# A weight split with every second low half made by an accumulating transfer: one decoder layer on one core

## The chip, the core and the metric

The kernel runs on one core of a Trainium2 chip. Its engines have queues of their own: TensorE (PE, with the weight loads shown apart as PEld), VectorE (DVE), ScalarE (ACT), GpSimd (POOL) and SyncE (SP), and 16 DMA engines serve the core. The metric is the device time of one execution in microseconds, as the median of the runs shown.

## What is computed

One layer of a decoder on x (256 positions, 2048 channels), all in float32:

```python
z = x @ w_in + b_in                      # 2048 x 15368
zu, zv, zqk, zvm, zo, zi, zf, zqx, zg = jnp.split(z, IN_OFFSETS, axis=-1)
y_a = chunked_spatial_gating(gelu(zu), gelu(zv), ...)
y_b = sigmoid(zo) * head_norm(mlstm(silu(conv(zqk)), zvm, zi, zf)) * m_norm_g
y_c = memory_cross_attention(zqx, mem_n @ x_w_kv)
merged = sum(sigmoid(zg_i) * (y_i @ w_pi) for i in (a, b, c))
x = layer_norm(ALPHA * x + merged @ w_out, ln1_g, ln1_b)
gate, up = jnp.split(x @ w_gu, 2, axis=-1)   # d_ff = 5632
x = layer_norm(ALPHA * x + (silu(gate) * up) @ w_down, ln2_g, ln2_b)
```

Nearly all of the work is products of the 256 positions with large weight matrices, some 331 MB of weights in float32.

## The kernel before

**Split products.** Each float32 operand of a large product is split into a high half in the format fp32r and a low half, the rest, in fp32r too. A product is then three: high by high, high by low, low by high. Activations are split once, where they are made. Weights are split as they stream in.

**Pieces and jobs.** All weights are cut into pieces of 256 rows by 512 columns, held as a tile of 128 x 1024 (512 KB). A job is one block of 512 columns: 4, 8 or fewer pieces, summed in PSUM, then evacuated. There are 632 pieces in one list, numbered through in the order of the jobs. In form A (`mul_a`, L1018) the weights are stationary: for each half `hf` four matmuls of the high half over both activation halves (L1024), then four of the low half over the high activations (L1026). In form B (`mul_b`, L1002) the weights move: for each of two row blocks and two channel blocks a matmul with the high half (L1014), one with the low half (L1015), one with the high half again (L1016). So the low half is wanted first behind four matmuls in form A, behind one in form B.

**The stream.** The order on each engine is the program's own. The loop over the pieces (L1092) calls, for piece i, `advance` (loads up to eight pieces ahead, L951, from SP), `advance_split` (the high half of piece i+4 and the low half of piece i+3), `mults(i)`, and at a job's end its evacuation; in between `run_side` adds steps of the side tasks (memory norm, gating, attention, mLSTM). A raw tile (`raw`, 6 buffers) is split in two instructions: `split` copies it to the high half `wh` on ScalarE (L979, 5 buffers), `split_lo` subtracts the high half from it on VectorE into `wl` (L994, 4 buffers). A high half can be made once the matmuls of the piece five before are done; then its buffer is free.

**Around it.** Evacuations (`comb`, L585, and the `ev_` functions) alternate between ScalarE and VectorE, and splits of new activations (`split_from`, L184) do too: ScalarE copies, VectorE subtracts. The high halves stand in ScalarE's queue behind these. GpSimd makes constants at the start, one mask (L282), and four small fills (L673). The output projection's last block and the last down projection (`late`) run one row block over their last pieces first, then the other, so that the row norms (`RowNorm`) can start; the last of their pieces have buffers of their own (`own`).

Of the kernel before, what the change touches and what calls it, by code (L numbers as in the profile page):

```python
# [12 lines left out]
F32R = mybir.dt.float32r  # L13
I32 = mybir.dt.int32
AF = mybir.ActivationFunctionType
ALU = mybir.AluOpType
# [3 lines left out]
P = 128  # L20
# [5 lines left out]
H = 4  # L26
ALPHA = 2.0 ** 0.25
EPS = 1e-5
RAW_BUFS = 6
HL_BUFS = 4  # L30
SPLIT_AHEAD = 3
LOAD_AHEAD = 8
SIDE_NS = 1000
VERBOSE = False
W0, W1 = 7, 14
# [53 lines left out]
def layer_kernel(ctx: ExitStack, tc: tile.TileContext, xT_d, mem_d, memT_d, wi_d, wif_d, wkv_d,  # L89
                 wpa_d, wpb_d, wpc_d, wout_d, wgu_d, wdn_d, pp_d, bif_d, gws_d, gbs_d, bin_d, gln_d, xr_d, lnp_d, out_d):  # L90
    nc = tc.nc
    ve, ac, te, gp, sy = nc.vector, nc.scalar, nc.tensor, nc.gpsimd, nc.sync
# [4 lines left out]
    wp = ctx.enter_context(tc.tile_pool(name="wp", bufs=HL_BUFS))  # L97
# [7 lines left out]
    def nm(s):  # L105
        cnt[0] += 1
        return f"{s}{cnt[0]}"

    def slot(tag, shape, dt=F32):
        return big.tile(shape, dt, tag=tag, name=nm(tag))  # L110
# [73 lines left out]
    def split_from(src, hi_ap, lo_ap):  # L184
        ac.activation(hi_ap, src, AF.Copy)  # L185
        ve.tensor_sub(lo_ap, src, hi_ap)  # L186
# [19 lines left out]
    def run_side(budget):  # L206
        held = False
        for t in list(tasks):
            if not t.free:
                if held:  # L210
                    continue
                held = True
            while budget > 0:
                try:
                    c = next(t.gen)
                except StopIteration:
                    tasks.remove(t)
                    break
                if c == WAIT:
                    break  # L220
                budget -= c
            if budget <= 0:
                break
# [723 lines left out]
    raw, hl, owned, cur = {}, {}, {}, [0]  # L947
# [3 lines left out]
    def load(i):  # L951
        job, k = pieces[i]
        r = wp.tile([P, 1024], F32, tag="raw", name=nm("raw"), bufs=RAW_BUFS)
        raw[i] = r
        if i == 0:
            for j in range(2):
                sy.dma_start(xraw[:, j], xT_d[:, j])
                sy.dma_start(r[:, j * 512:(j + 1) * 512], job.src[k][:, j * 512:(j + 1) * 512])
            return
        if i < nx:  # L960
            sy.dma_start(xraw[:, 2 * i:2 * i + 2], xT_d[:, 2 * i:2 * i + 2])
        sy.dma_start(r, job.src[k])
        if k == 0 and job.bias is not None:
            job.bc = bc2()
            o = job.bias
            sy.dma_start(job.bc, bin_d[0:1, o:o + 512].to_broadcast([P, 512]))

    def split(i):
        job, k = pieces[i]
        r = raw[i]  # L970
        if k in job.own:
            tag, m = job.own[k]
            if m == 0:
                S["own"] = slot(tag, [P, 2, 2, 1024], F32R)
            h = S["own"][:, m, 0]
            owned[i] = S["own"][:, m, 1]
        else:
            h = wp.tile([P, 1024], F32R, tag="wh", name=nm("wh"), bufs=HL_BUFS + 1)
        ac.activation(h, r, AF.Copy)  # L979
        hl[i] = [h, None]  # L980

    def split0():
        r = raw.pop(0)
        h = wp.tile([P, 1024], F32R, tag="wh", name=nm("wh"), bufs=HL_BUFS + 1)
        l = wp.tile([P, 1024], F32R, tag="wl", name=nm("wl"))
        hl[0] = [h, l]
        for j in range(2):
            o = slice(j * 512, (j + 1) * 512)
            split_from(xraw[:, j], xT.one(j, 0), xT.one(j, 1))
            split_from(r[:, o], h[:, o], l[:, o])  # L990

    def split_lo(i):
        l = owned.pop(i) if i in owned else wp.tile([P, 1024], F32R, tag="wl", name=nm("wl"))
        ve.tensor_sub(l, raw.pop(i), hl[i][0])  # L994
        hl[i][1] = l

# [67 lines left out]
    def advance(i):  # L1064
        while state["ld"] < min(N, i + LOAD_AHEAD + 1) and state["ld"] < state["sp"] + RAW_BUFS:
            load(state["ld"])
            if state["ld"] == 2:
                sy.dma_start(pp, pp_d)
            state["ld"] += 1

    def advance_split(i):
        while state["sp"] < min(N, i + SPLIT_AHEAD + 1):
            k = state["sp"]
            while state["hi"] < min(N, k + 2):
                if state["hi"] == 0:
                    split0()
                else:
                    if state["hi"] < nx:
                        xsplit_hi(state["hi"])
                    split(state["hi"])  # L1080
                state["hi"] += 1
            if k > 0:
                if k < nx:
                    xsplit_lo(k)
                split_lo(k)
            state["sp"] += 1
            advance(i)
# [4 lines left out]
    for i in range(N):  # L1092
        job, k = pieces[i]
# [13 lines left out]
        else:  # L1107
            run_side(SIDE_NS)

# [61 lines left out]
```

## Time and profile before

| | |
|---|---|
| median of three runs | 1864.68 us (1863.83 to 1866.85) |
| the profiled execution: its own time | 1864.04 us |
| span in the profile, first to last instruction | 1862.3 us |
| PE busy | 1840.6 us |
| VectorE busy | 1148.7 us |
| ScalarE busy | 898.4 us |
| GpSimd busy | 4.4 us |
| mean granted clock of TensorE | 0.996 |
| DMA | 351.53 MB, mean 189 GB/s |

Busy time is the union of an engine's instructions. An engine that is busy less than the span may still set its length, if others wait for it in turn; the chain that ended last tells which. The granted clock is a share of 2.4 GHz; the lower level is 1.2 GHz. A DMA share is the mean share of time in which the 16 DMA engines had packets under way.

### The profile page before, as it was taken

What the parts mean: (1) busy time and instruction counts of PE and PEld (TensorE: products, weight loads), DVE (VectorE), ACT (ScalarE), POOL (GpSimd) and SP (SyncE); (2) the same over time, 40 slices, a digit from 0 to 9 for tenths busy, and PEclk for the clock granted to TensorE, in tenths of its full rate; (3) what the DMA queues carried; (4) which work ended last, traced back from release to release, by engine and by line L of the source; (5) the groups of instructions that cost most, each with busy time, mean ns of one, the idle gap of its engine ahead of it and who ended that gap; (6) DMA issues with size and microseconds to landing.
All of it is one profiled execution on the core that took longest, in us unless ns stands there. A gap on an engine that the chain in (4) does not pass through costs nothing.

```text
span 1862.3 us, 25100 instructions
## 1 busy us (share of the span) xinstructions
PE 1840.6 (99%) x9796; PEld 1568.3 (84%) x9796; DVE 1148.7 (62%) x1434; ACT 898.4 (48%) x1045; POOL 4.4 (0%) x18
## 2 busy tenths in 40 slices
PE   9999999999999999999999989999999999999997
PEld 8888888888888888888888878888888888888885
DVE  6786566556767666655555568555555555555557
ACT  6554456545555555544444455443443443444442
POOL 0000000000000000000000000000000000000000
PEclk9999999999999999999999999999999999999998
DMA  9666555555555555565556635656555555556572
GB/s 360 220 223 193 182 161 177 171 160 186 176 183 172 169 180 169 181 195 190 183 190 231 233 122 173 197 187 192 186 187 190 185 190 183 185 190 189 185 236 90
DMA packets 97478, 351.53 MB, mean 189 GB/s; under 512 B 10832, under 2 KB 11344, under 8 KB 96336
## 3 DMA queue, kind: packets, MB, share of 16 engines
q1 hardware_dynamic: 97360, 349.94, 57.2%
q8 instruction: 76, 1.25, 0.3%
q14 instruction: 42, 0.34, 0.1%
HBM read 347.80 MB, written 2.10 MB: 188 GB/s over the span
## 4 chain that ended last, share of the span: by engine, by line
PE 97%; DVE 2%; ACT 1%; DMA 0%; issue 0%; SPq 0%; ACTq 0%
PE acc L1024 45%; PE acc L1026 23%; PE acc L1016 9%; PE acc L1015 9%; PE acc L1014 9%; PE tr L180 1%; PE tr L181 0%; PE tr L182 0%; DMA raw<-in_wi 0%; DVE s L747 0%; DVE wl L994 0%; DVE s L743 0%; DVE rst L725 0%; DVE t L797 0%; PE tr L404 0%
## 5 line engine op out<-in xcount | busy, mean ns | idle before, releaser
L994 DVE TENSOR_TENSOR wl<-raw,wh 128x1024 fp32r<-128x1024 f32 x625 | 759.0, 1223 | 477.8 <-PE acc L1026 311.7
L979 ACT ACTIVATE wh<-raw 128x1024 fp32r<-128x1024 f32 x625 | 653.9, 1057 | 681.9 <-PE acc L1024 384.8
L1024 PE MATMUL acc<-s,wh 128*128 128x512 f32 x3520 | 969.1, 397 | 0.6 <-ACT wh L185 0.5
L1024 PEld LDWEIGHTS acc<-s,wh 128*128 128x128 f32 x3520 | 602.2, 188 | 82.0 <-ACT wh L185 0.8
L1026 PEld LDWEIGHTS acc<-s,wl 128*128 128x128 f32 x3520 | 543.5, 190 | 81.0 <-DVE wl L994 0.5
L1026 PE MATMUL acc<-s,wl 128*128 128x256 f32 x3520 | 561.9, 282 | 0.1
L1016 PE MATMUL acc<-wh,s 128*128 128x512 f32 x680 | 270.5, 398 | 0.0
L1014 PE MATMUL acc<-wh,s 128*128 128x512 f32 x680 | 268.4, 395 | 0.8 <-DVE s L759 0.8
L1015 PE MATMUL acc<-wl,s 128*128 128x512 f32 x680 | 267.8, 394 | 0.0
L1015 PEld LDWEIGHTS acc<-wl,s 128*128 128x128 f32 x680 | 127.7, 188 | 31.6
L1014 PEld LDWEIGHTS acc<-wh,s 128*128 128x128 f32 x680 | 127.7, 188 | 30.7 <-DVE s L759 1.2
L1016 PEld LDWEIGHTS acc<-wh,s 128*128 128x128 f32 x680 | 127.6, 188 | 30.2
L592 DVE TENSOR_TENSOR g<-g,acc 128x512 f32<-128x512 f32 x54 | 37.1, 688 | 50.9 <-ACT g L591 34.6
L840 DVE TENSOR_TENSOR s<-s,acc 128x512 f32<-128x512 f32 x38 | 24.6, 684 | 28.2 <-PE acc L1016 28.2
L591 ACT ACTIVATE g<-acc,pp 128x256 f32<-128x256 f32 x64 | 26.8, 470 | 28.9 <-PE acc L1026 28.9
L592 DVE TENSOR_TENSOR t<-t,acc 128x512 f32<-128x512 f32 x38 | 26.0, 684 | 13.7 <-ACT t L588 13.7
L588 ACT ACTIVATE t<-acc 128x512 f32<-128x512 f32 x38 | 22.4, 591 | 19.0 <-PE acc L1026 19.0
L185 ACT ACTIVATE s<-g 128x512 fp32r<-128x512 f32 x22 | 13.9, 632 | 33.9 <-DVE g L828 33.9
L186 DVE TENSOR_TENSOR s<-g,s 128x512 fp32r<-128x512 f32 x22 | 15.2, 692 | 15.4 <-ACT s L185 15.4
L486 DVE SCALAR_TENSOR_TENSOR t<-g,pp,t 128x256 f32<-128x256 f32 x48 | 23.3, 485 | 2.0
L592 DVE TENSOR_TENSOR s<-s,acc 128x512 f32<-128x512 f32 x20 | 13.7, 687 | 15.8 <-ACT s L588 9.4
L588 ACT ACTIVATE g<-acc 128x512 f32<-128x512 f32 x22 | 13.2, 598 | 18.0 <-PE acc L1026 18.0
(256 smaller groups left out, 786.9 us busy)
## 6 DMA issues: line engine op xcount, KB each, us to landing
raw<-in_wi SPq DMA_DIRECT2D x239, 512.0 KB, 3.6
raw<-in_wgu SPq DMA_DIRECT2D x176, 512.0 KB, 4.1
raw<-in_wdn SPq DMA_DIRECT2D x88, 512.0 KB, 4.2
raw<-in_wkv SPq DMA_DIRECT2D x32, 512.0 KB, 3.8
raw<-in_wpb SPq DMA_DIRECT2D x32, 512.0 KB, 4.4
raw<-in_wout SPq DMA_DIRECT2D x32, 512.0 KB, 4.1
raw<-in_wpa SPq DMA_DIRECT2D x16, 512.0 KB, 3.6
raw<-in_wpc SPq DMA_DIRECT2D x16, 512.0 KB, 4.0
```

Of the source, the lines that this page charges most:

```text
L486: ve.scalar_tensor_tensor(y, zc[:, c, k:k + T], pv(f"cw{k}", j), y, ALU.mult, ALU.add)
L588: ac.activation(out, ps[:, :, T:2 * T], AF.Copy)
L591: ac.activation(out[:, c], ps[:, c, T:2 * T], AF.Identity, bias=pv(bias[0], bias[1] + 2 * hf + c))
L592: ve.tensor_add(out, out, ps[:, :, 0:T])
L840: ve.tensor_add(a, a, ps)
L979: ac.activation(h, r, AF.Copy)
L994: ve.tensor_sub(l, raw.pop(i), hl[i][0])
L1014: te.matmul(ps, a.sta(kt, 0, t), wh, start=f, stop=False)
L1015: te.matmul(ps, a.sta(kt, 0, t), wl, start=False, stop=False)
L1016: te.matmul(ps, a.sta(kt, 1, t), wh, start=False, stop=e)
L1024: te.matmul(ps, w[:, o:o + P], a.both(kt), start=k == 0 and j == 0, stop=False)
L1026: te.matmul(ps[:, 0:T], w[:, o:o + P], a.hi(kt), start=False, stop=k == job.n - 1 and j == 1)
```

## The change

From piece 32 on, every even piece gets its low half in another way. ScalarE writes the negated high half into the low half's tile, right behind the high half, and a transfer issued from GpSimd then adds the piece's weights from HBM onto it: low = weights - high. VectorE's subtraction is left out for these pieces, and their raw tile is given up once the high half is made. The weights of these pieces are thus read from HBM twice. The raw tiles go from 6 buffers to 5, the low halves from 4 to 5.

```diff
-RAW_BUFS = 6
+RAW_BUFS = 5
 HL_BUFS = 4
...
+DMA_LO = 32
...
         ac.activation(h, r, AF.Copy)
         hl[i] = [h, None]
+        if by_dma(i):
+            l = owned.pop(i) if i in owned else lo_tile()
+            ac.activation(l, h, AF.Identity, scale=-1.0)
+            gp.dma_start(l, job.src[k], accum_op=ALU.add)
+            raw.pop(i)
+            hl[i][1] = l
+
+    def by_dma(i):
+        return i >= DMA_LO and i % 2 == 0
+
+    def lo_tile():
+        return wp.tile([P, 1024], F32R, tag="wl", name=nm("wl"), bufs=HL_BUFS + 1)
 
     def split0():
...
-        l = wp.tile([P, 1024], F32R, tag="wl", name=nm("wl"))
+        l = lo_tile()
...
     def split_lo(i):
-        l = owned.pop(i) if i in owned else wp.tile([P, 1024], F32R, tag="wl", name=nm("wl"))
+        if hl[i][1] is not None:
+            return
+        l = owned.pop(i) if i in owned else lo_tile()
         ve.tensor_sub(l, raw.pop(i), hl[i][0])
         hl[i][1] = l
```

## Rows read from the trace of the kernel before

**Rows 1.** The page: span, busy time of each engine, the chain that ended last.

```profile
span 1862.3 us, 25100 instructions
...
PE 1840.6 (99%) x9796; PEld 1568.3 (84%) x9796; DVE 1148.7 (62%) x1434; ACT 898.4 (48%) x1045; POOL 4.4 (0%) x18
...
PE 97%; DVE 2%; ACT 1%; DMA 0%; issue 0%; SPq 0%; ACTq 0%
```

**Rows 2.** Windows of 25 us: busy us (instructions) by engine, PE clock, DMA share, GB/s.

```profile
25.00:50.00 25.00, 25.00 (x143) 21.75 (x142) 15.82 (x17) 14.85 (x18) 0.00 (x0) 1.00 1.00 392
...
1100.00:1125.00 25.00, 22.55 (x123) 19.56 (x124) 17.64 (x26) 15.46 (x23) 0.00 (x0) 0.90 0.31 99
1125.00:1150.00 25.00, 25.00 (x144) 21.79 (x144) 22.95 (x27) 12.98 (x14) 0.00 (x0) 1.00 0.61 204
...
1350.00:1375.00 25.00, 25.00 (x145) 21.77 (x144) 11.94 (x11) 11.19 (x13) 0.00 (x0) 1.00 0.57 187
```

**Rows 3.** The page's costliest groups: the subtraction and the high half; busy, mean ns.

```profile
L994 DVE TENSOR_TENSOR wl<-raw,wh 128x1024 fp32r<-128x1024 f32 x625 | 759.0, 1223 | 477.8 <-PE acc L1026 311.7
L979 ACT ACTIVATE wh<-raw 128x1024 fp32r<-128x1024 f32 x625 | 653.9, 1057 | 681.9 <-PE acc L1024 384.8
```

**Rows 4.** The tile raw: duration of an issue (ns), and issue to landing (us).

```profile
L962 SPq DMA_DIRECT2D raw<-in_wgu x176: 327/328/328, 1067.0 to 1755.9; - x176
...
DMA to landing us min/median/max: 3.3/4.1/10.2
```

**Rows 5.** POOL in order of time, after the start: start, us, instruction, idle before.

```profile
125.36 1.89 POOL L282 TENSOR_SCALAR_AFFINE_SELECT wT<-wT 128x1024 f32<-128x1024 f32 x1 [122.46 <-DMA wT<-in_gws]
352.09 0.11 POOL L673 MEMSET g<- 128x12 f32 x1 [224.84 <-DVE s L654]
441.47 0.11 POOL L673 MEMSET g<- 128x12 f32 x1 [89.28 <-DVE s6b L186]
```

**Rows 6.** Timeline of an ordinary piece: high halves, and the first low-half matmuls.

```profile
1276.36 1.06 ACT L979 ACTIVATE wh<-raw 128x1024 fp32r<-128x1024 f32 x1 [1.74 <-PE acc L1016]
1279.16 1.06 ACT L979 ACTIVATE wh<-raw 128x1024 fp32r<-128x1024 f32 x1 [1.74 <-PE acc L1016]
...
1288.28 0.63 PE L1026 MATMUL acc<-s,wl 128*128 128x256 f32 x4
```

**Rows 7.** Timeline at the short places and the tail, the same two engines.

```profile
871.02 0.63 ACT L185 ACTIVATE s<-s 128x512 fp32r<-128x512 f32 x1 [2.32 <-DVE s L659]
871.56 3.89 ACT L979 ACTIVATE wh<-raw 128x1024 fp32r<-128x1024 f32 x4
...
878.21 0.64 PE L1026 MATMUL acc<-s,wl 128*128 128x256 f32 x4
...
1006.92 2.94 ACT L979 ACTIVATE wh<-raw 128x1024 fp32r<-128x1024 f32 x3
...
1012.79 0.39 PE L1015 MATMUL acc<-wl,s 128*128 128x512 f32 x1
...
1156.43 2.94 ACT L979 ACTIVATE wh<-raw 128x1024 fp32r<-128x1024 f32 x3
...
1164.53 0.64 PE L1026 MATMUL acc<-s,wl 128*128 128x256 f32 x4
...
1246.67 3.07 ACT L979 ACTIVATE wh<-raw 128x1024 fp32r<-128x1024 f32 x3
...
1253.99 0.39 PE L1015 MATMUL acc<-wl,s 128*128 128x512 f32 x1
...
1825.81 1.04 ACT L979 ACTIVATE s<-raw 128x1024 fp32r<-128x1024 f32 x1
...
1833.28 0.40 PE L1015 MATMUL acc<-s,s 128*128 128x512 f32 x1
```

**Rows 8.** VectorE behind the first LayerNorm: the four subtractions between 1104 and 1118.

```profile
1104.99 1.22 DVE L994 TENSOR_TENSOR wl<-raw,wh 128x1024 fp32r<-128x1024 f32 x1
...
1109.65 1.22 DVE L994 TENSOR_TENSOR wl<-raw,wh 128x1024 fp32r<-128x1024 f32 x1
...
1113.68 1.22 DVE L994 TENSOR_TENSOR wl<-raw,wh 128x1024 fp32r<-128x1024 f32 x1
...
1117.18 1.22 DVE L994 TENSOR_TENSOR wl<-raw,wh 128x1024 fp32r<-128x1024 f32 x1
```

## The prediction

> **What bounds the kernel now.** I read the page's first section first: PE is busy 1840.6 of 1862.3 us, VectorE (DVE) 62%, ScalarE (ACT) 48% [rows 1]. A busy PE need not be at its peak, so next the chain that ended last: 97% of it is PE, 2% VectorE, 0% DMA, so almost no step of the span waits for the operation that the diff removes [rows 1]. Third, the windows: a 25 us stretch of form A (16 matmuls a piece) holds 143 to 145 matmuls, with VectorE busy 11.94 us or 22.95, and with DMA at 187 GB/s or at 392 [rows 2]. PE's pace answers to neither. One piece takes PE 2.80 us (ScalarE's next high half starts 2.80 us after the last [rows 6]) or some 2.82 (25 us by 144 matmuls, times 16, is 2.78). Only the stretch from 1100 to 1125 shows PE short, 22.55 of 25 us at a granted clock of 0.90, that is between its two levels, behind idle gaps of the first LayerNorm [rows 2].
>
> So freeing VectorE can't pay much; the change is decided by whether the new low halves arrive before PE wants them.
>
> **What it removes.** 300 pieces (the even ones from 32 to 630 of 632) lose their subtraction: 300 x 1.22 us = 367 us of VectorE [rows 3]. Its cover is PE, so this gains nothing outside the LayerNorm stretch. There, two of the four subtractions between 1104 and 1118 [rows 8] go, at most 2 x 1.22 = 2.4 us; I count 0, since the units between them wait for ScalarE and transposes too.
>
> **What it adds to ScalarE.** A negation of the size and form of the high half, 1.06 us [rows 3], 300 times: 318 us, which takes ScalarE from 898 to 1216 us of 1862, 65%. PE hides the sum. What isn't hidden is its place: the negation stands between the high half and the transfer that needs it, so each of the 300 low halves starts 1.06 us later, and a high half queued behind it in a run moves by as much (its price is looked at below).
>
> **Buffers.** The raw tiles go from 6 to 5, but an even piece's raw tile now falls free when ScalarE has read it, not when VectorE has subtracted. The low halves get a fifth buffer, so an odd subtraction may run a piece earlier than now, and frees its raw tile earlier too. A load still leaves some four pieces (4 x 2.8 = 11.2 us) ahead of its high half, less the 2.3 us of the two steps that free its slot; it lands in 4.1 us as a median and 10.2 at worst [rows 4]. Cost 0; with the cover gone (a load over 9 us) each late one costs its excess.
>
> **What it adds to POOL.** 300 transfers go into a queue that works in order. Before, that queue was free to wait; its other work after the start is one mask of 1.89 us and four fills of 0.11 us [rows 5]. The mask is emitted in the iteration of piece 40 and ran at 125.36; piece 46, the next even piece behind it in the queue, has its high half made only at about that time (its turn comes when piece 41 is done), so nothing waits. A fill waits for a buffer whose last reader, the split of the value projection (or, for the first, a product of projection a), stands at least a job of 8 pieces earlier in the program, so it finds it free. Cost 0; each transfer held up there would eat into the time of the next part.
>
> **What it adds to DMA.** 300 x 0.524 MB = 157 MB more from HBM, 508 MB in all, 273 GB/s against 392 GB/s that the engines reached at a share of 1.00 [rows 2]. The trace has no accumulating transfer. Per pair of pieces (5.60 us) two loads take 2 x 1.34 us at 392 GB/s, so 2.92 us are left. Lower bound: an accumulation costs what a load does, 1.34 us. Upper: it reads its destination too, and at the 328 GB/s that 187 at a share of 0.57 stand for: 3.20 us, with loads at 1.60. I take two reads at 392, 2.67 us, nearest to the row with full engines: it fits, with 0.25 us to spare. The Trainium skill (Collectives: The Full Stack, "The bandwidth ceiling: the fold count and why AG ≠ RS ≠ AR") says that an add in the DMA path costs not for the arithmetic but because it reads two sources, about halving the rate; no run here shows it yet. By it the term is the 2.67 us that I take, by the load's row alone 1.34.
>
> **The time that each has.** This is the term that counts. For each of the 300 pieces I laid the end of its high half on ScalarE beside the start of the first matmul that reads its low half. An ordinary piece: high half from 1276.36 to 1277.42, low half wanted at 1288.28: 10.86 us [rows 6], and half of all have 10.9 or more. But ScalarE falls behind where a job is evacuated. Its splits wait some 2.2 us for three VectorE operations, and the high halves come in a run afterwards; the first of the run, five pieces behind the evacuated job's last, is the late one. Four kinds are short [rows 7]:
> - behind branch b's projection: 872.61 (871.56 plus 1.05) to 878.21, 5.60 us; three pieces
> - behind its last block, where form B follows: 1007.96 to 1012.79, 4.83 us; one piece
> - behind an up projection, where a down projection follows: 1247.72 to 1253.99, 6.27 us; five pieces
> - behind an up projection, where a gate projection follows: 1157.48 to 1164.53, 7.05 us; six pieces
>
> and at the tail three pieces have 7.37, 6.43 (1826.85 to 1833.28) and 5.76 us. The other 282 have over 7.8 us.
>
> **How long the low half takes.** After the high half: 1.06 us of negation, then L from issue to landing. Lower bound of L: a load's 4.1 us, SP's 0.33 us of issue included [rows 4]. On top come POOL's making of the descriptors, between 0 and a whole POOL pass over a tile of this size, 1.89 us [rows 5], and the second read, between 0 and 1.34. The far bound is 10.2 us, the slowest load, issued among others at the start. I take 4.1 + 0.95 (half of 1.89) + 1.34 = 6.4 us, so a piece needs 7.46. A stall that has been taken delays PE, so the next two even pieces have that much more; only the tail's three are that near. The shift within a run adds nothing yet: the closest case, two pieces behind the 4.83, ends its high half with the run at 1009.86 and is wanted at 1012.79 + 2 x 2.80, 8.53 us later; less 1.06 it keeps 7.47. Sum: 3 x 1.86 + 2.63 + 5 x 1.19 + 6 x 0.41 + 1.70 (tail) = 18.3 us. Likewise L = 4.1 gives 0.3, 5.2 gives 3.9, 8.7 gives 89 (54 pieces) and 10.2 gives 181 (94 pieces).
>
> The profiled execution took 1864.04 us, 0.64 under the median of the runs shown. 1864.04 + 18.3 = 1882.3, and with the 0.64, 1883.
>
> **Rivals.**
> - Hidden: L up to 5.2 us, stalls under 3.9 us, time 1864.7 to 1868.6. For it: the median load at 4.1, and 11.2 us of lead on most pieces. Against: no part of an accumulation is cheaper than a load, and two parts come on top. It decides at 5.2 us. The Trainium skill (DMA: Bandwidth & Descriptors, "Anatomy of one DMA — SWDGE (gpsimd) path") fits a transfer from this queue as 2.0 us plus bytes by 436 GB/s. An estimate from it is 3.2 us for 0.52 MB and 4.4 with two reads, which would make this rival the outcome; loads here run 0.9 us over the former [rows 4].
> - DMA too slow: L over 8.7 us, or over 2.92 us of all engines per accumulation. With the upper bound a pair needs 2 x 1.60 + 3.20 = 6.40 us for 5.60: 300 x 0.80 = 240 us, so 2105; by latency alone 1954 (L = 8.7) to 2045 (L = 10.2). For it: the margin of 0.25 us is thin, and a load leaves at the very moment at which the high half frees its slot, so both share the engines. Against: the engines are at 0.57 in the steady state [rows 2].
> - Faster: the LayerNorm stretch. PE loses 2.45 us there to gaps and up to 0.10 x 25 = 2.5 us to the clock [rows 2]. If the two subtractions that go all stood on its path, 2.4 us, and PE regained the clock sooner, up to 4.9 us come back and L up to 4.1 costs 0.3: 1860. It decides at both subtractions and over half of the clock's loss. Against: VectorE is 2% of the chain.
>
> **How the numbers follow.** 0.2% is 3.7 us, about what a measurement of this kernel tells from no change. Forecast (L from 5.2 to 8.7, 1868 to 1954, its own range): 0.46. Hidden: 0.24. DMA too slow: 0.22. Faster: 0.08. So faster 0.08, same 0.24, slower 0.46 + 0.22 = 0.68. The range starts at 1861, since hiding must be held and a small gain with it, and ends at 2045, the far bound of L; beyond it lies the throughput case, about 0.12, and below it some 0.06.
>
> **What the profile after would show.** Right: VectorE's subtraction 331 times instead of 631 and its busy time down by some 367 us; ScalarE's busy time up by 318; accumulating transfers landing 6.4 us after issue as a median; PE's pace unchanged at 2.8 us a piece; PE waiting for transfers at the short places alone, longest behind branch b's projection. Wrong: landings at 5 us or less with no PE wait at the short places (hidden); PE waits at most even pieces, spread over the whole span, or a DMA share near 1.00 (too slow). A stall that pulls the granted clock down for longer, POOL held up in its own issue, or high halves that ScalarE makes late in new places would each add time that this sum lacks.

## The result, and the profile after

The kernel with the change takes 1976.27 us as a median (1972.72 to 1979.85, four runs) against 1864.26 us of the kernel before beside it: 1.06 times the time, 95% interval 1.0587 to 1.0613, or 112 us more. The forecast was 1883, slower, with stalls of 18.3 us. The direction and the range hold; the size is off by a factor of six.

The page of the profiled execution (1975.9 us):

```profile
span 1974.2 us, 25466 instructions
...
PE 1876.0 (95%) x9796; PEld 1579.6 (80%) x9796; DVE 794.4 (40%) x1134; ACT 1208.7 (61%) x1345; POOL 259.2 (13%) x318
...
q1 hardware_dynamic: 97360, 349.94, 49.1%
q0 software_dynamic: 43200, 157.31, 43.0%
...
PE 51%; DMA 20%; issue 18%; DVE 2%; ACT 1%; POOL 0%; POOLq 0%; ACTq 0%
...
L1009 DVE TENSOR_TENSOR wl<-raw,wh 128x1024 fp32r<-128x1024 f32 x328 | 400.7, 1222 | 638.3 <-PE acc L1041 335.4
...
L984 ACT ACTIVATE wl<-wh 128x1024 fp32r<-128x1024 f32 x297 | 315.0, 1060 | 9.4
```

Lines have shifted: the high half is L980, the negation L984, the transfer L985, the subtraction L1009; form A's matmuls are L1039 and L1041, form B's L1029 to L1031. Beside [rows 1] and [rows 3]: the work has moved as forecast, with VectorE 354 us less busy and ScalarE 310 us more, and the remaining subtractions cost the same 1.22 us each. But PE's share of the chain has fallen from 97% to 51%, and DMA stands in it with 20%, through the tile `wl`; the 18% of `issue` are time in which an engine of the chain waited for nothing that the profile shows.

Two differences add up to the whole loss. PE is idle for 1974.2 - 1876.0 = 98.2 us, where it was 1862.3 - 1840.6 = 21.7 before: 76.5 more. And it is busy for 35.4 us more with the same 9796 matmuls. 76.5 + 35.4 = 111.9 us, the difference of the spans. The first part is in the waits of PE (us in total, times, longest):

```profile
PE acc L1041 <- DMA wl<-in_wi: 19.5, 14, 3.7
PE acc L1041 <- DMA wl<-in_wgu: 19.5, 15, 2.5
PE acc L1030 <- DMA wl<-in_wdn: 18.9, 8, 5.3
PE acc L1030 <- DMA wl<-in_wout: 8.9, 4, 3.6
PE tr L792 <- ACT t L782: 4.0, 4, 1.8
PE acc L1030 <- DVE wl L1009: 3.2, 1, 3.2
PE tr L792 <- DVE t L798: 2.1, 1, 2.1
...
PE acc L1041 <- DMA wl<-in_wpb: 1.5, 3, 0.8
```

Five of these lines are matmuls that read a low half and wait for its transfer: 68.3 us in 44 waits; with two single waits of the kind that are left out here it is 69.2 us in 46. One line is an odd piece, whose subtraction came 3.2 us late: ScalarE had stood 6.55 us for a load (its wait ends at 1036.83), and the steps behind it came late. The other two are the first LayerNorm's transposes, with about what they had before (3.6 and 2.1). How long the transfer takes, from its issue to its landing (shortest, median, longest), is in the last line of the view of the tile `wl`, here followed by that of the loads into `raw` (L963):

```profile
DMA to landing us min/median/max: 5.8/8.4/11.6
```

```profile
DMA to landing us min/median/max: 3.3/6.9/18.8
```

The forecast's L was 6.4. It is 8.4 as a median, and the loads have gone from 4.1 to 6.9 [rows 4].

One short place in order of time, the first of the three behind branch b's projection (start, us, instruction, idle before; three engines):

```profile
889.14 1.04 ACT L980 ACTIVATE wh<-raw 128x1024 fp32r<-128x1024 f32 x1
890.22 1.06 ACT L984 ACTIVATE wl<-wh 128x1024 fp32r<-128x1024 f32 x1
...
891.57 0.84 POOL L985 DMA_DIRECT2D wl<-in_wi  x1 [10.61 <-ACT wl L984]
...
893.44 1.10 PE L1039 MATMUL acc<-s,wh 128*128 128x512 f32 x4
894.38 0.64 PE L1041 MATMUL acc<-s,wl 128*128 128x256 f32 x4
894.86 1.09 PE L1039 MATMUL acc<-s,wh 128*128 128x512 f32 x4
899.69 1.22 PE L1041 MATMUL acc<-s,wl 128*128 128x256 f32 x4 [3.74 <-DMA wl<-in_wi]
900.71 1.91 PE L1039 MATMUL acc<-s,wh 128*128 128x512 f32 x4
```

The high half is done at 890.18, and PE has finished the four matmuls ahead of the low half at 895.95: an allowance of 5.77 us (forecast 5.60, [rows 7]). The negation ends at 891.28, the transfer is issued 0.29 us later, and PE goes on at 899.69, 8.1 us after the issue. Up to the gap PE keeps its pace of 1.41 us per half piece, 2.82 a piece. Behind it the same four low-half matmuls take 1.22 instead of 0.64 us, and the next four high-half ones 1.91 instead of 1.10. That is most of the second part of the loss. The longest gap shows it at length (PE alone, form B; then 5 us windows with PE's busy time, the weight loads, the other engines, granted clock, DMA share and GB/s):

```profile
1894.64 0.40 PE L1031 MATMUL acc<-wh,s 128*128 128x512 f32 x1
1894.88 0.39 PE L1029 MATMUL acc<-wh,s 128*128 128x512 f32 x1
1900.58 0.79 PE L1030 MATMUL acc<-wl,s 128*128 128x512 f32 x1 [5.31 <-DMA wl<-in_wdn]
1901.17 0.63 PE L1031 MATMUL acc<-wh,s 128*128 128x512 f32 x1
1901.60 0.63 PE L1029 MATMUL acc<-wh,s 128*128 128x512 f32 x1
...
1905.87 0.59 PE L1030 MATMUL acc<-wl,s 128*128 128x512 f32 x1
1906.29 0.40 PE L1031 MATMUL acc<-wh,s 128*128 128x512 f32 x1
```

```profile
1890.00:1895.00 5.00, 5.00 (x23) 3.93 (x21) 1.22 (x1) 3.83 (x4) 1.70 (x2) 1.00 0.79 256
1895.00:1900.00 5.00, 0.27 (x2) 0.00 (x0) 2.42 (x3) 2.11 (x2) 0.84 (x1) 0.94 1.02 301
1900.00:1905.00 5.00, 4.42 (x10) 3.47 (x11) 0.00 (x0) 0.00 (x0) 0.00 (x0) 0.50 1.04 284
1905.00:1910.00 5.00, 5.00 (x20) 4.00 (x19) 0.35 (x1) 1.21 (x2) 0.00 (x0) 0.87 1.04 348
```

Behind the gap the matmuls start 0.43 us apart, at the 1.2 GHz level (granted clock 0.50), until 1906; before it and later they start 0.235 us apart. The 13 steps from the start at 1900.58 to that at 1906.29 take 5.71 us, where they would take 13 x 0.235 = 3.06. So a gap of 5.3 us costs 2.65 us more after its end. Not every gap does this: of the 17 gaps of over 2 us outside the LayerNorm the lower level stands behind twelve; behind the other five, of 2.2 to 2.8 us, the clock stayed at 1.00.

Over the span the mean granted clock is 0.983 (0.996 before). That is (1 - 0.983) x 1974.2 - (1 - 0.996) x 1862.3 = 26 us more that are lost to the lower level, gaps included, so the clock can't be all of the 35.4 us. Counted in the trace start by start, the matmuls at the lower level with no gap before them come 24.4 us later than at full pace, 1.8 us before the change: 22.6 of the 35.4 us. Some 8 more are part of the waits: a matmul's record lasts 0.39 us, the next one's start is 0.235 us behind its own, so the first 0.16 us of each wait count as busy, and PE's waits are 59 instead of 11. The last 5 us aren't settled.

### The profile page after: what moved, and what is told of

Read it like the earlier page. It is cut to its first block, busy times and chain, and to the rows that moved or that the text cites. A ratio compares the mean times of both kernels' runs of the same rounds, so it can differ in the third digit from the quotient of the medians.

```text
span 1974.2 us, 25466 instructions
## 1 busy us (share of the span) xinstructions
PE 1876.0 (95%) x9796; PEld 1579.6 (80%) x9796; DVE 794.4 (40%) x1134; ACT 1208.7 (61%) x1345; POOL 259.2 (13%) x318
## 3 DMA queue, kind: packets, MB, share of 16 engines
q1 hardware_dynamic: 97360, 349.94, 49.1%
## 4 chain that ended last, share of the span: by engine, by line
PE 51%; DMA 20%; issue 18%; DVE 2%; ACT 1%; POOL 0%; POOLq 0%; ACTq 0%
PE acc L1039 21%; PE acc L1041 12%; DMA wl<-in_wi 6%; DMA wl<-in_wgu 6%; PE acc L1030 6%; PE acc L1031 5%; PE acc L1029 5%; DMA wl<-in_wdn 4%; DMA wl<-in_wout 1%; DMA wl<-in_wpb 1%; DMA s<-in_wout 0%; DMA wl<-in_wkv 0%; POOL wl L985 0%; PE tr L181 0%; ACT wh L980 0%
## 5 line engine op out<-in xcount | busy, mean ns | idle before, releaser
L1039 PE MATMUL acc<-s,wh 128*128 128x512 f32 x3520 | 974.2, 398 | 3.6 <-ACT wh L980 1.6
L980 ACT ACTIVATE wh<-raw 128x1024 fp32r<-128x1024 f32 x625 | 654.3, 1055 | 509.9 <-PE acc L1039 303.7
L1039 PEld LDWEIGHTS acc<-s,wh 128*128 128x128 f32 x3520 | 605.5, 189 | 85.8 <-ACT wh L980 1.8
L1009 DVE TENSOR_TENSOR wl<-raw,wh 128x1024 fp32r<-128x1024 f32 x328 | 400.7, 1222 | 638.3 <-PE acc L1041 335.4
L1041 PEld LDWEIGHTS acc<-s,wl 128*128 128x128 f32 x3520 | 544.5, 191 | 135.8 <-DMA wl<-in_wi 27.9
L1041 PE MATMUL acc<-s,wl 128*128 128x256 f32 x3520 | 569.7, 284 | 41.0 <-DMA wl<-in_wi 19.5
L984 ACT ACTIVATE wl<-wh 128x1024 fp32r<-128x1024 f32 x297 | 315.0, 1060 | 9.4
L1030 PE MATMUL acc<-wl,s 128*128 128x512 f32 x680 | 276.1, 406 | 31.6 <-DMA wl<-in_wdn 18.9
L1029 PE MATMUL acc<-wh,s 128*128 128x512 f32 x680 | 273.5, 402 | 0.8 <-DVE s L760 0.8
L1031 PE MATMUL acc<-wh,s 128*128 128x512 f32 x680 | 272.9, 401 | 0.0
L985 POOL DMA_DIRECT2D wl<-in_wi x104 | 88.8, 854 | 634.1 <-ACT wl L984 432.8
L1029 PEld LDWEIGHTS acc<-wh,s 128*128 128x128 f32 x680 | 130.3, 192 | 32.3 <-DVE s L760 1.2
L1031 PEld LDWEIGHTS acc<-wh,s 128*128 128x128 f32 x680 | 131.0, 193 | 31.0
L985 POOL DMA_DIRECT2D wl<-in_wgu x88 | 74.9, 852 | 466.0 <-ACT wl L984 415.7
L593 DVE TENSOR_TENSOR g<-g,acc 128x512 f32<-128x512 f32 x54 | 37.1, 688 | 124.3 <-ACT g L592 77.5
L985 POOL DMA_DIRECT2D wl<-in_wdn x42 | 35.8, 851 | 231.4 <-ACT wl L984 211.2
L593 DVE TENSOR_TENSOR t<-t,acc 128x512 f32<-128x512 f32 x38 | 26.0, 683 | 67.5 <-ACT t L589 67.5
L841 DVE TENSOR_TENSOR s<-s,acc 128x512 f32<-128x512 f32 x38 | 24.6, 683 | 70.7 <-PE acc L1031 70.7
L589 ACT ACTIVATE t<-acc 128x512 f32<-128x512 f32 x38 | 22.5, 591 | 18.1 <-PE acc L1041 18.1
```

The source lines that it names most:

```text
L593: ve.tensor_add(out, out, ps[:, :, 0:T])
L841: ve.tensor_add(a, a, ps)
L984: ac.activation(l, h, AF.Identity, scale=-1.0)
L985: gp.dma_start(l, job.src[k], accum_op=ALU.add)
L1029: te.matmul(ps, a.sta(kt, 0, t), wh, start=f, stop=False)
L1030: te.matmul(ps, a.sta(kt, 0, t), wl, start=False, stop=False)
```

## The experiments

Three theories stood after the result. **Latency:** one accumulation takes longer than a short place allows, and the clock falls behind each gap. **Throughput:** the DMA engines can't carry 509 MB in the time. **Another part:** the negation on ScalarE, the buffers or the order of queues. Each median stands against the kernel before on the same chip (1864.26 to 1864.65).

**1. The parts without the transfers** (`bufs`, `neg`). The first keeps only the buffers. The second keeps the buffers and the negations; VectorE then adds the raw tile, and nothing is transferred.

```diff
 def by_dma(i):                                  # bufs
-    return i >= DMA_LO and i % 2 == 0
+    return False
...
     ac.activation(l, h, AF.Identity, scale=-1.0)   # neg
-    gp.dma_start(l, job.src[k], accum_op=ALU.add)
-    raw.pop(i)
...
 def split_lo(i):
     if hl[i][1] is not None:
+        ve.tensor_add(hl[i][1], hl[i][1], raw.pop(i))
         return
```

> Only the buffers of the change: 5 raw tiles, 5 low halves, every low half by VectorE. All theories that blame the transfers: 1862 to 1868. Fewer raw tiles as the cause: above 1875, with ScalarE or VectorE waiting for loads.

> Buffers and negations of the change, no transfers: ScalarE writes the negated high half for the 300 pieces, VectorE then adds the raw tile onto it in place, so the work on VectorE is that of the kernel before. Late low halves: 1864 to 1870. ScalarE's added 318 us as a cause of its own (the 26 us that remained where PE didn't wait for the transfers): 1885 or more.

Measured: 1864.43 us (1.0001, 0.9992 to 1.0011) and 1865.26 (1.0004, 0.9995 to 1.0014). The page of the second:

```profile
PE 1840.3 (99%) x9796; PEld 1567.6 (84%) x9796; DVE 1147.2 (62%) x1434; ACT 1208.4 (65%) x1345; POOL 3.7 (0%) x18
```

ScalarE carries the whole 310 us of negations, and PE is as busy as before. Buffers and negations cost nothing that can be measured; the 112 us come with the transfers.

**2. The wait taken away** (`nowait`).

```diff
             gp.dma_start(l, job.src[k], accum_op=ALU.add)
             raw.pop(i)
-            hl[i][1] = l
+            hl[i][1] = h[:, :]
```

> All of the change, transfers, negations and buffers included, but the low-half matmuls of the 300 pieces read the high half's tile, so PE never waits for an accumulation; the product of the true low half is left out for these pieces. Late low halves (PE waits for single accumulations at the short places, 70 us, and the clock falls behind those stalls): 1864 to 1875 us, DMA share still 0.9 or more, accumulations still landing after some 8 us. Full DMA engines (loads and accumulations need more engine time than a pair of pieces has, so the loads fall behind): 1940 us or more, PE waiting for high halves and these for raw tiles. ScalarE too loaded (negations delay high halves and evacuations): 1890 us or more, PE waiting for ScalarE.

Measured: 1890.35 us (1.0134, 1.0118 to 1.0149). The transfers still run and land as late (median 8.4), but no matmul waits for them: 86 of the 112 us are gone, all that hung on that wait, its clock loss included. 26 us are left, more than the 0 to 10 that the expectation had for late low halves; 1890 is the bound that it gave for a ScalarE too loaded, and `neg`, with the same work on ScalarE, shows that this work alone costs nothing. The page, PE's waits, ScalarE's waits for loads, and ScalarE around the longest of PE's waits:

```profile
span 1883.7 us, 25569 instructions
...
PE 1845.7 (98%) x9796; PEld 1570.2 (83%) x9796; DVE 794.6 (42%) x1134; ACT 1208.3 (64%) x1345; POOL 259.3 (14%) x318
...
q1 hardware_dynamic: 97360, 349.94, 50.4%
q0 software_dynamic: 43200, 157.31, 44.2%
```

```profile
PE acc L1030 <- DVE wl L1009: 8.0, 3, 7.0
```

```profile
ACT wh L980 <- DMA raw<-in_wdn: 39.0, 19, 8.5
ACT wh L980 <- DMA raw<-in_wout: 33.4, 10, 9.8
ACT wh L980 <- DMA raw<-in_wgu: 22.1, 15, 2.2
```

```profile
1012.57 1.06 ACT L980 ACTIVATE wh<-raw 128x1024 fp32r<-128x1024 f32 x1 [9.78 <-DMA raw<-in_wout]
```

ScalarE stood 9.78 us for a load; the high halves, the evacuations and the subtraction behind it came late, and PE waited 7.0 us for an odd piece's subtraction. The loads of this kernel land in 7.8 us as a median, 18.8 at worst. The two queues hold the engines for 50.4% + 44.2% = 94.6% of the span; per pair of pieces that is 2 x 1.42 us of loads (0.504 x 1883.7 / 667.5, 349.94 MB being 667.5 tiles) and 2.78 of the accumulation (0.442 x 1883.7 / 300), 5.62 us for PE's 5.60. So with the low-half waits gone the engines are just about full, and ScalarE waits 94.5 us for loads of these three matrices, for which it has no wait in the kernel before. One late load that stops PE is shown; that all of the 26 us are such loads is argued from these shares and waits, not shown.

**3. Half of the accumulations** (`mod4_0`, `mod4_2`). All even pieces at which a short place begins are divisible by four, two of the tail's three apart.

```diff
-        return i >= DMA_LO and i % 2 == 0
+        return i >= DMA_LO and i % 4 == 0     # mod4_0;  mod4_2: i % 4 == 2
```

> Only every fourth piece, those with a number divisible by 4, gets its low half by a transfer: 150 accumulations, half of the traffic, but all short places except two at the tail are among them. Late low halves: L from issue to landing falls with the traffic to some 7 us, the gaps are 30 to 50 us, time 1900 to 1930. Full DMA engines: half of the accumulations leave the engines at a share of some 0.75, so the slowdown all but goes, 1864 to 1872.

> Also every fourth piece, but those with a remainder of 2: the same 150 accumulations and the same traffic, off the short places (tail pieces 626 and 630 apart). Late low halves: gaps of 2 to 9 us, time 1864 to 1876, and at least 20 us under the run with remainder 0. Full DMA engines: the same time as the run with remainder 0, within 5 us.

Measured: 1954.03 us (1.0482, 1.0459 to 1.0505) and 1900.55 (1.0195, 1.018 to 1.0211). The two move the same bytes, so the places decide: 150 transfers that hold all the short ones but two at the tail keep 89 of the 112 us, 150 beside them 36. Both times lie above what was expected for late low halves. For full engines the first should have been 1864 to 1872 and the second the same within 5 us, so throughput is not the main cause. The first one's queues and its tile `wl`:

```profile
q1 hardware_dynamic: 97360, 349.94, 51.2%
q0 software_dynamic: 21600, 78.65, 22.7%
```

```profile
DMA to landing us min/median/max: 5.6/7.9/11.4
```

The engines are held 74% instead of 92% of the time, and an accumulation lands half a microsecond earlier. In the second, 27.6 us of gaps stand before its low halves. Its landings are 6.7, 8.1 and 11.9 (shortest, median, longest); it is the late ones that stop PE at pieces whose allowance the median would keep.

**4. The second read taken out** (`plain`): the same transfer, without the accumulation.

```diff
-            gp.dma_start(l, job.src[k], accum_op=ALU.add)
+            gp.dma_start(l, job.src[k])
```

> The change with the 300 transfers from GpSimd made plain copies instead of accumulations: the low half's tile gets the weights themselves, so the subtraction of the high half is left out for these pieces. Same queue, same bytes from HBM, no read of the destination. If the second read is what makes an accumulation late, the median from issue to landing falls from 8.4 to some 5.5 us (a 4 KB row takes 159 ns in a load and 327 ns in an accumulation), PE's gaps at these pieces to under 15 us, and the time to 1870 to 1890. If GpSimd's queue itself is slow, landing stays at 7.5 us or more and the time at 1930 or more.

Measured: 1899.48 us (1.0189, 1.0174 to 1.0205), above the 1870 to 1890 that were expected; the landing fell to 6.4 us, not to 5.5. Its page and its tile `wl`:

```profile
PE 1852.1 (98%) x9796; PEld 1571.4 (83%) x9796; DVE 794.8 (42%) x1134; ACT 1208.4 (64%) x1345; POOL 162.1 (9%) x318
...
q0 software_dynamic: 43200, 157.31, 25.4%
```

```profile
DMA to landing us min/median/max: 3.8/6.4/10.0
```

By chance this run is the forecast's own case, L = 6.4: the gaps before these low halves are 22.5 us at 17 pieces, where the forecast had 18.3 us at 18. Even so it loses 35 us; the granted clock is 0.992, so part of the other 13 is the clock again. An accumulation holds all engines for 0.430 x 1974.2 / 300 = 2.83 us, this copy for 0.254 x 1898.0 / 300 = 1.61, and the landing differs by 2.0 us. Part of that is the lighter load on the engines: `mod4_0`, whose queues hold them for about the same share (74%, here 77%), has 7.9 us, 1.5 more than the plain copy. GpSimd's instruction is shorter too (259.2 against 162.1 us for about 300).

**5. The transfer sent earlier** (`negfirst`): the negation is made from the raw tile, ahead of the high half.

```diff
-        ac.activation(h, r, AF.Copy)
         hl[i] = [h, None]
         if by_dma(i):
...
-            ac.activation(l, h, AF.Identity, scale=-1.0)
+            ac.activation(l, r, AF.Identity, scale=-1.0)
...
             hl[i][1] = l
+        ac.activation(h, r, AF.Copy)
```

> The change with ScalarE's two instructions turned round: the negation reads the raw tile, stands ahead of the high half, and the transfer leaves 1.06 us earlier. Late low halves: every piece has 1.06 us more, the gaps fall from 70 us to some 35 and with the clock's share the time to 1910 to 1940. Full engines or ScalarE's load: the same work and bytes, so 1970 to 1980.

Measured: 1911.35 us (1.0253, 1.0238 to 1.0268), 65 us less than the change, with the same landings (5.5, 8.4, 12.7) and the same bytes. One microsecond per transfer moves more than half of the loss; with a limit of throughput the expectation was no change (1970 to 1980).

**6. The first of each run spared** (`skip`): the 90 pieces whose high half opens a run go back to VectorE; 210 transfers stay.

```diff
-        return i >= DMA_LO and i % 2 == 0
+        return i >= DMA_LO and i % 2 == 0 and pieces[i - 5][1] != pieces[i - 5][0].n - 1
```

> The change without the 90 pieces that stand five behind the end of a job; 210 accumulations are left, 70% of the added bytes. Late low halves: the gaps fall from 70 us to under 20 and the time to 1868 to 1895. A cost of the traffic as such would leave 70% of the loss, 1940 or more.

Measured: 1910.62 us (1.0244, 1.0228 to 1.0259), above what was expected. There are 33 us of gaps left, at 25 pieces. Sixteen of these are the next accumulated pieces of the same runs, with landings of 9.3 to 12.0 us, against a median of 8.4 in this run as well. In the kernel before such a piece has some 3.7 us more than the first of its run (9.34 against 5.60 us behind branch b's projection), so it is mostly the late landing that holds it up. Sparing the first alone is not enough; why the next transfer of a run lands late is not shown.

**7. Splits ahead of evacuations** (`early`), so that no run forms.

```diff
         if k == job.n - 1:
             if not job.late:
+                if i + 1 < N:
+                    advance(i + 1)
+                    advance_split(i + 1)
                 job.evac(job)
```

> The change with one order turned: at a job's end the next high half, its negation and its transfer are emitted ahead of the evacuation instead of behind it, so that ScalarE makes them before its run of splits. Late low halves: the short places get 3 to 6 us back; PE's gaps at accumulated pieces fall from 70 us to under 25, time 1870 to 1900. Full DMA engines: no change, 1960 to 1980, since the same bytes move. ScalarE too loaded: no change or slower, since evacuations wait longer.

Measured: 2003.19 us (1.0755, 1.0727 to 1.0782), a miss. The waits for low halves fell as expected (to 20 us), but PE's largest waits are now these:

```profile
PE acc L1039 <- DVE g L593: 40.3, 23, 2.0
PE acc L1039 <- DVE t L593: 21.5, 13, 1.7
PE acc L1039 <- DVE s L593: 12.8, 8, 1.9
```

L593 is VectorE's part of an evacuation, which now stands behind the splits; the next job's matmuls wait for its PSUM.

**8. The clock by itself** (`fill`): spare matmuls, whose result nothing reads, ahead of the sixteen pieces with the longest gaps.

```diff
+        if i in SHORT:     # 292, 308, 324, 340, 348, 354, 404, 420, 452, 468, 500, 516, 548, 564, 596, 612
+            b = bank()
+            for _ in range(16):
+                te.matmul(b[:, 0:P], ones, ones, start=True, stop=True)
         mults(i)
```

> The change with 16 spare matmuls of 128 columns (1.9 us) in front of each of the 16 pieces whose gap was longest; they do no useful work and fill part of PE's wait. If the time beyond the gaps (36 of 112 us) is the clock that falls behind a long gap, PE's granted clock rises, and the time falls to 1945 to 1968. If it is something else, the time stays at 1974 or rises by up to 16 x 1.9 = 30 us.

Measured: 1966.11 us (1.0547, 1.053 to 1.0564), 10 us less than the change. Its page and the group of the spare matmuls:

```profile
span 1962.5 us, 26491 instructions
...
PE 1912.8 (97%) x10308; PEld 1624.5 (83%) x10308; DVE 794.3 (40%) x1134; ACT 1208.8 (62%) x1345; POOL 259.2 (13%) x318
```

```profile
L1119 PE MATMUL tr<-ones 128*128 128x128 f32 x512 | 60.1, 276 | 0.0
```

60.1 us of useless work went in, and the kernel became faster. PE's idle time fell by 48.5 us (98.2 to 49.7), which the spare work fills; the kernel's own matmuls took 1912.8 - 60.1 = 1852.7 us, 23.3 less than in the change; +60.1 - 48.5 - 23.3 = -11.7, the difference of the spans. The mean granted clock went from 0.983 to 0.993. Counted in the trace as above, the matmuls at the lower level come 6.9 us late instead of 24.4, so 17.5 of the 23.3 us are the clock; the gaps are also fewer and shorter.

**9. The best of these together** (`fewest`): `negfirst`, and only pieces with `i % 4 == 2`.

> Every fourth piece with remainder 2 (150 accumulations, off the short places), with the negation and the transfer ahead of the high half: 1.06 us more than in the run with remainder 2, which had 28 us of gaps. Late low halves: gaps under 12 us, 1868 to 1882. Not below the kernel before, since PE sets the span there.

Measured: 1870.45 us (1.0032, 1.0021 to 1.0042). Seven pieces still wait, for 5.4 us in all. It is the fastest of the versions that keep the transfers, and still 0.3% slower than the kernel before: VectorE's freed time buys nothing, so each wait is a loss.

## Why the prediction was off

**What bounds the kernel: right.** 354 us less of VectorE brought nothing, and the LayerNorm's waits stayed as they were, so the rival "faster" is out. One reading of the prediction was wrong here: the stretch from 1100 to 1125 is not the only one that shows PE short. The stretch before it, from 1075 to 1100, has PE busy for 20.97 of 25 us, so that rival had 4 us more to win than it was given; the waits stayed all the same.

**Zero for ScalarE's sum, the buffers and GpSimd's order: right.** `neg` and `bufs` show the first two; for the third, no wait of PE in the change names the mask or the fills. Piece 46's transfer did stand behind the mask, issued at 131.08, some 2 us after its negation, but PE did not wait for it.

**The places: right.** Three pieces behind branch b's projection wait 3.74, 3.49 and 2.37 us; the first of its last block 3.60; five behind an up projection with a down projection next 2.15 to 5.31; and six before a gate projection, 1.30 to 2.47. These fifteen have 41.7 us, where the forecast gave them 16.6 and its formula with the measured L gives 46.6. Of the tail's three, priced at 1.70 together, the first waited, though it was the one with the most time (7.37 us):

```profile
1941.98 0.50 PE L1030 MATMUL acc<-wl,s 128*128 128x512 f32 x1 [1.78 <-DMA wl<-in_wdn]
```

The other two did not; that stall gave them time, and their transfers landed in 6.9 and 5.4 us. The remaining 25.7 us of the 69.2 are at 30 places that the forecast's L of 6.4 had spared.

**The step that failed is "How long the low half takes".** L was 4.1 + 0.95 + 1.34 = 6.4 us; it measured 8.4. The three summands came from a quiet kernel. The first two gave 5.05 us for a transfer from GpSimd's queue without the second read; it takes 6.4 (`plain`), 1.2 us more than a load in the same run (5.2), and the loads had already slowed from 4.1 to 5.2. The second read, taken as 1.34, adds 2.0 us between `plain` and the change, and 1.5 at about the same share of the engines (`mod4_0`). So most of the missing 2.0 us go with the load on the engines that the change itself brings. From the end of the negation to the issue another 0.3 us pass, which the sum left out. Behind 1.06 us of negation this acts like an L of 8.7, for which the forecast's own table had 89 us; measured are 69.2, of them 60.6 at the 54 pieces of that table. The table credits a stall to the next pieces already; what makes the rest is that the transfers at these 54 pieces landed in 7.9 us as a median, not 8.4, and for 7.9 + 0.3 the same rule gives 66 us. The pieces that are too short grow so fast in number (18 at 6.4, 54 at 8.7) that 2.3 us of L change the stalls nearly fourfold.

**The term that was missing is the clock.** It was named at the end as something that the sum lacks. Most gaps of 2 to 5 us are followed by matmuls at the 1.2 GHz level, and 35.4 us of busier PE came on top of 76.5 us of idle. The trace puts 22.6 of them to the lower level, and `fill` shows that filling the gaps takes most of that back (24.4 to 6.9). Some 8 are the beginnings of the waits, counted as busy; 5 aren't settled.

**The pair's DMA time.** Taken were 2 x 1.34 + 2.67 = 5.35 us for 5.60; measured are 2 x 1.45 + 2.83 = 5.73, so it doesn't quite fit. The rule of the Trainium skill (Collectives: The Full Stack, "The bandwidth ceiling: the fold count and why AG ≠ RS ≠ AR"), that an add in the DMA path costs by its two sources, agrees with the trace: 2.83 against 1.61 us, 1.76 times. But throughput is the smaller part, as `mod4_0` against `mod4_2` and `negfirst` show; it bears on the 26 us that `nowait` leaves open. The fit of the Trainium skill (DMA: Bandwidth & Descriptors, "Anatomy of one DMA — SWDGE (gpsimd) path"), from which the rival "hidden" had 3.2 and 4.4 us, does not hold beside this stream of loads: 6.4 and 8.4 as medians, 3.8 and 5.8 at the shortest.

## What to carry to other kernels

A step that is moved behind a transfer must be held against the shortest allowance on the path, not the usual one, and where many places lie just above the forecast latency, a small error of it becomes a large one of the time. Take the latency for a queue that is loaded as it will be after the change: here the change slowed its own transfers and the loads. The median isn't enough either: right behind a run the transfers landed in some 10 us, not 8.4 (`skip`). And where stalls stop TensorE for some microseconds each, they can cost more than their length: here 76 us of gaps brought 23 us of lower clock behind them.

## What was not expected of the hardware

- Half as many accumulations hardly shorten one: 8.4 us at a DMA share of 92%, 7.9 at 74%; the shortest of all is still 5.8 and 5.6.
- GpSimd's issue of an accumulating transfer takes 0.85 us, of a plain one of the same shape 0.53.
- Sixty microseconds of useless matmuls in the gaps made the kernel 10 us faster.
